# Hybrid DeltaNet/MLA/MoE block: one-pass products in the router's waits, rotary keys doubled by DMA, the decays' series with one instruction a term

## Chip, cores and metric

One Trainium2 chip, one core. The metric is the device time of one execution in microseconds, as the median of the runs. Engines are named as in the profile: PE is TensorE, PEld its weight loads, DVE is VectorE, ACT is ScalarE, POOL is GpSimd, SP is SyncE, which issues most DMAs.

## What is computed

A block of a bidirectional encoder over 512 tokens of 1024 features, in fp32: a gated DeltaNet (8 heads, both directions, chunks of 64) and a latent attention (MLA, 8 heads) side by side, merged by sigmoid gates, then a mixture of 16 experts in which each expert takes its 64 highest-scoring tokens. Cut to what the change touches:

```python
# MLA: one rotary key for all heads
q = rms_norm(c_q, q_gain) @ w_uq
k_rope = apply_rope(k_r, cos, sin)
# DeltaNet: decay per token and head
g = -exp(a_log) * softplus(a + dt_bias)          # cumulated within a chunk, then exp(differences)
# experts choose tokens
aff = softmax(h @ w_router)
gate, idx = top_k(aff.T, 64)                     # per expert
xe = h[idx]
hid = silu(xe @ w_gate) * (xe @ w_up)
ye = (hid @ w_down) * gate
out = zeros.at[idx].add(ye)
```

## The kernel before

Everything lies transposed, features on partitions and 512 tokens along the free axis, so that one product of 128 weights by 512 tokens fills a PSUM bank. A product at high accuracy is `mm3`: both factors are split into a high and a low part (ACT writes the high part, DVE or POOL the low one) and three one-pass products are accumulated. Where an operand is plain fp32, one product shows as two instructions in the trace.

The framework fixes the order of each engine's queue when the kernel is built: among what it thinks ready, the instruction that is earlier in the program goes first. Each engine works through its queue in that order. Tiles of one name take turns in a fixed number of buffers, in program order; the default PSUM bank `mm` has two. `tc.issue_after(ins)` puts what is traced under it behind `ins` on the same engine. Under `tc.manual_schedule` an engine keeps the order of the program.

The stages in order of time, with the lines that the prediction steps through:

- **Latents and rotary key (L283 to L412).** `lat_half` projects the latents; L321 and L322 take the square root on ACT and the reciprocal on DVE for the key-value norm, L324 applies it. L330 writes the low half of the query latent `cq`. `kr_ps` (L338) holds the projected key (64 rows) and the DeltaNet's a and b (32 rows); ACT copies all 96 rows to `kr1` (L340) and sends the last 32 to DRAM (L342). L348 sums the squares `sqs` over partitions, ACT copies the sums to `rs` (L350), four transposes (L353) turn them into a column per token. Then a product with `twice` (two identities side by side, L343 to L345 and L363) writes the 64 key rows twice into a second `kr_ps`, because the rotary helper `rope` (L397) works on 128 rows. `stage_a` (L432) projects the queries of two heads, the rotary part first (L452).
- **Attention (L519).** Heads go through `stage_a`, `stage_b` and `stage_c`, one step apart.
- **DeltaNet projections (L685).** For keys, then queries: projection, convolution on DVE (L667, L669), Silu on ACT (L670). After the sixth key tile comes `decays` (L590): softplus by a series in L612 to L620, then `gu` (L628), which eight small products (L632) read.
- **Decay blocks (L745).** For each of four token tiles `t` and both types `ty`: POOL multiplies (L749), PE applies `Lbd` (L751, bank `pjb`), ACT exponentiates; then the products `gkq` (L765). The framework merges them into the query projections.
- **Inverses, chunk steps, merge, output projection (L777 to L1300).**
- **Router (L1180 to L1377).** For each token tile `t`, while the next tile's output projection runs: transposes, logits with a fold product (`sum`, L1201), softmax, a transpose of the scores (L1227), then eight rounds of max and replace on DVE (`largest`). For the last tile PE has nothing else to do. `thr16` (L1324) is transposed (L1355), compared, and `counts` gives each token its place by bf16 products with `upto` and `ones_b`. `group` writes the one-hot tiles `OG` (L1393), `gather` multiplies them with the tokens (L1408).
- **Experts (L1543 on).** Weights come in quarters of 1 MB through a ring of 17 buffers (`ring`, L990); once the ring is full, the next load waits for the products that read the oldest quarter. The loops at L1543 and L1555 run gate, up and down products for the 16 experts.

Of the kernel before, what the change touches and what calls it, by code (L numbers as in the profile page):

```python
# [40 lines left out]
def block_kernel(ctx: ExitStack, tc: tile.TileContext, x, c, positions, w_mod, b_mod, g_mix, w_in, conv_w,  # L41
# [45 lines left out]
    def mm(o, lhsT, rhs, start=True, stop=True):  # L87
        return pe.matmul(o, lhsT, rhs, start=start, stop=stop)  # L88

    def mm3(o, lh, ll, rh, rl, start, stop):  # L90
# [251 lines left out]
    act.dma_start(ba_d, kr1[64:96])  # L342
    twice = mp("twice", 128)  # L343
    for i in range(2):
        dve.tensor_copy(twice[:64, 64 * i:64 * i + 64], ident[:64, :64])  # L345
    ss = lat[0]
    for i in range(4):
        mm(ss[32 * i:32 * i + 32], ones[:, 0:32], sqs[:, i])  # L348
    rs = tmp("rs", "t1")
    act.activation(rs, ss, AF.Copy)  # L350
    ss = lat[1]
    for t in range(4):
        turned_ = pe.transpose(ss[:, 128 * t:128 * t + 128], rs[:, 128 * t:128 * t + 128], ident)  # L353
    scq = mp("scq", 4)
# [5 lines left out]
    pm = Region("pmla", space=PSUM)  # L360
    kr_ps = bank("kr")
    with tc.issue_after(turned_.ins):
        mm(kr_ps, twice[:64], kr1[:64])  # L363

# [43 lines left out]

    kr = rope(kr_ps, True)
    tap("kr", kr)  # L410
# [179 lines left out]
    def decays():  # L590
# [24 lines left out]
        dve.tensor_tensor(t_[3], t_[2], t_[2], op=OP.mult)  # L615
        dve.tensor_scalar(t_[4], t_[3], 1.0 / 17, 1.0 / 15, op0=OP.mult, op1=OP.add)
        for n in (13, 11, 9, 7, 5, 3, 1):
            dve.tensor_tensor(t_[4], t_[4], t_[3], op=OP.mult)
            dve.tensor_scalar(t_[4], t_[4], 1.0 / n, None, op0=OP.add)
        dve.tensor_tensor(t_[4], t_[4], t_[2], op=OP.mult)  # L620
        dve.scalar_tensor_tensor(t_[4], t_[4], 2.0, t_[1], op0=OP.mult, op1=OP.add)
# [123 lines left out]
    for t in range(4):  # L745
        Dt = []
        for ty in range(2):
            gM = dp("gM", 512, bufs=2)
            pool.tensor_tensor(h8(gM), bh8(Mpk[ty]), b64(gu[:, ty, t]), op=OP.mult)  # L749
            psd = bank("pjb", 1, pp_)  # L750
            mm(psd, Lbd[ty], gM)  # L751
            Dx, Di = dp("Dx", 512, bufs=4), dp("Di", 512, bufs=4)
# [6 lines left out]
        for g in range(2):  # L759
            pv = bank("gkq", 2, pp_).rearrange("p (h e n) -> p h e n", h=4, e=2)  # L760
            hs = slice(4 * g, 4 * g + 4)
            for h in range(4):
                for cc in range(2):
                    q = slice(64 * cc, 64 * cc + 64)
                    mm(pv[q, h], kf[4 * g + h][:, t, cc], kq[4 * g + h][:, t, 2 * cc:2 * cc + 2][:, ::1 - 2 * cc])  # L765
            for e in range(2):
                for ty in range(2):
                    D_ = h8(Dt[ty][e])
                    dst = nAv(ty, t) if e == 0 else D_
                    dve.tensor_tensor(dst[:, hs], pv[:, :, e], D_[:, hs], op=OP.mult)  # L770
# [409 lines left out]
    class Logits:  # L1180
# [20 lines left out]
        def sum(self):  # L1201
            lT = dp("lT", 128)
            act.copy(lT, self.lg[:, :128])
            mm(self.lg[:, 128:144], lT, fold)
            return self.lg[:, 128:144]
# [5 lines left out]
    def scored(t):  # L1211

        a, m, s_, r_ = aff[:, t, :], stt[:, t, 0:1], stt[:, t, 1:2], stt[:, t, 2:3]
        lg = L[t].sum()
        act.activation(tbl[:, 1:2], rs[:, t:t + 1], AF.Exp, scale=0.0)
        dve.scalar_tensor_tensor(a, lg, rs[:, t:t + 1], c16, op0=OP.mult, op1=OP.add)
# [9 lines left out]
        pa = L[t].lg[:16, 256:384]  # L1226
        pe.transpose(pa, a, ident)  # L1227
        if t == 2:
# [131 lines left out]
    dve.tensor_tensor(eq, aff, b4(pth[:, :16]), op=OP.is_equal)  # L1360

    def counts(v, w=None):

# [6 lines left out]
        for i, (c, l, r) in enumerate(terms):  # L1370
            mm(ps[:, c], l, r, i == 0, i == len(terms) - 1)
        return ps[:, :64].rearrange("p (t e) -> p t e", t=4)
# [67 lines left out]
    for j in range(2):  # L1440
        ahead[j] = halves_of(j)
    group(0)
    gather(0, 0, 1)
    gather(0, 1, 1)
# [239 lines left out]
```

## Time and profile before

| | us |
|---|---|
| median of 3 runs | 1306.71 |
| lowest and highest run | 1306.16, 1306.81 |
| the profiled execution | 1305.51 |
| its span, first to last instruction | 1303.7 |
| PE busy in the span | 1225.3 (94%) |
| DVE, ACT, POOL busy | 668.7, 473.4, 314.5 |
| HBM read | 308.42 MB |

Times in the rows are microseconds from the start of the span unless marked ns. A timeline row gives start, duration, engine, line, operation, output and inputs, shape, and a count where neighbours of one kind are merged; in square brackets stands the idle time before it and what ended it. L88 is the line of the product helper `mm`, so that its rows are told apart by their tiles. PE's matmuls overlap, so the spacing of starts says more than durations. PEclk is the clock granted to PE: 1.00 is 2.4 GHz, 0.50 is 1.2 GHz.

### The profile page before, as it was taken

The numbers are of one execution on the slowest core, as the hardware profiler recorded it, in microseconds if no ns is written. First come the engines' busy times: TensorE is split into PE (matmuls) and PEld (weight loads), VectorE is DVE, ScalarE is ACT, GpSimd is POOL, SyncE is SP. The second block draws the span as 40 slices with busy tenths as digits, with TensorE's granted clock in tenths as the row PEclk, the third lists the DMA queues.
The fourth block names the chain that finished last, engine by engine and source line by source line (L and its number), as shares of the span: only waits on it lengthen the run. The fifth ranks groups of instructions, "written<-read, shape, count | busy, mean of one in ns | idle before, by whom it ended". The sixth has DMA issues, their size and how long they took to land.

```text
span 1303.7 us, 18255 instructions
## 1 busy us (share of the span) xinstructions
PE 1225.3 (94%) x6911; PEld 767.0 (59%) x6911; DVE 668.7 (51%) x1306; ACT 473.4 (36%) x986; POOL 314.5 (24%) x264
## 2 busy tenths in 40 slices
PE   5999999999999999999999999699999999999895
PEld 3767777667667777777877776333433443343233
DVE  4577776475669925945686766412222312223125
ACT  4455655556533346335631336410201110021003
POOL 2221210233544452434332242300300110020003
PEclk9989999999999999999999999799999999999998
DMA  9421222754363578585489773799999999999995
GB/s 353 121 63 41 71 88 70 232 178 138 121 186 97 180 195 230 168 235 170 161 295 316 249 257 140 285 379 421 421 420 420 421 421 420 421 420 421 420 414 185
DMA packets 153842, 333.82 MB, mean 256 GB/s; under 512 B 44864, under 2 KB 104462, under 8 KB 128794
## 3 DMA queue, kind: packets, MB, share of 16 engines
q1 hardware_dynamic: 130048, 308.75, 64.1%
q10 hardware_dynamic: 23370, 23.50, 5.7%
q8 instruction: 54, 0.88, 0.3%
q0 software_dynamic: 336, 0.41, 0.2%
q14 instruction: 34, 0.28, 0.1%
HBM read 308.42 MB, written 24.20 MB: 255 GB/s over the span
## 4 chain that ended last, share of the span: by engine, by line
PE 34%; DMA 22%; DVE 4%; ACT 2%; issue 1%; POOL 0%; SPq 0%; DVEq 0%; ACTq 0%; POOLq 0%
PE mm L88 11%; DMA exw<-in_w_down_dram 8%; DMA exw<-in_w_gate_dram 6%; PE wg L88 5%; DMA exw<-in_w_up_dram 4%; PE dnp L88 3%; PE wu L88 3%; PE po L88 2%; PE sc L88 2%; PE I L88 2%; PE Y L88 1%; DMA kq<-kq_d 1%; PE Q L88 1%; PE S L88 1%; DMA wraw<-in_w_o_dn_dram 1%
## 5 line engine op out<-in xcount | busy, mean ns | idle before, releaser
L88 PE MATMUL mm<-hT,wh 128*128 128x512 f32 (+1 forms) x656 | 218.5, 410 | 2.8 <-ACT wh L99 2.1
L96 POOL TENSOR_TENSOR wl<-wraw,wh 128x512 fp32r<-128x512 f32 (+1 forms) x88 | 126.8, 1457 | 254.8 <-ACT wh L99 236.9
L88 PEld LDWEIGHTS mm<-hT,wh 128*128 128x128 f32 (+1 forms) x656 | 122.4, 191 | 43.0 <-issue 9.5
L88 PE MATMUL mm<-hT,wl 128*128 128x512 f32 (+1 forms) x328 | 133.3, 406 | 3.8 <-POOL wl L96 3.7
L99 ACT ACTIVATE wh<-wraw 128x512 fp32r<-128x512 f32 (+1 forms) x138 | 86.5, 650 | 120.1 <-PE mm L88 58.0
L88 PE MATMUL wg<-exw,xe 128*64 128x512 f32 x512 | 121.8, 602 | 3.8 <-DMA exw<-in_w_gate_dram 2.5
L88 PE MATMUL wu<-exw,xe 128*64 128x512 f32 x512 | 117.8, 598 | 1.9 <-DMA exw<-in_w_up_dram 1.9
L96 POOL TENSOR_TENSOR xl<-xs,xh 128x512 fp32r<-128x512 f32 x32 | 40.2, 1273 | 307.3 <-ACT xh L1384 307.3
L1541 DVE TENSOR_TENSOR ye<-dnp,gt 64x512 f32<-64x512 f32 x30 | 20.7, 689 | 134.1 <-PE dnp L88 118.2
L1482 DVE TENSOR_TENSOR xa<-sc,xa 128x512 f32<-128x512 f32 x56 | 38.5, 691 | 88.4 <-PE sc L88 88.4
L88 PEld LDWEIGHTS mm<-hT,wl 128*128 128x128 f32 (+1 forms) x328 | 62.4, 190 | 22.4 <-POOL wl L96 6.0
L88 PEld LDWEIGHTS wu<-exw,xe 128*64 128x64 f32 x512 | 34.6, 137 | 65.6 <-issue 56.1
L88 PEld LDWEIGHTS wg<-exw,xe 128*64 128x64 f32 x512 | 33.6, 137 | 65.7 <-issue 55.0
L96 DVE TENSOR_TENSOR wl<-wraw,wh 128x512 fp32r<-128x512 f32 (+2 forms) x50 | 40.0, 811 | 39.5 <-ACT wh L99 28.9
L88 PE MATMUL po<-W,am 128*128 128x512 f32 x192 | 50.3, 406 | 0.8 <-DVE W L96 0.6
L793 DVE TENSOR_TENSOR pr<-lanT,nl 128x1 f32<-128x1 f32 (+30 forms) x62 | 43.7, 704 | 1.6
L667 DVE SCALAR_TENSOR_TENSOR cv<-mm,vecT,cv 128x510 f32<-128x510 f32 (+1 forms) x32 | 23.8, 743 | 35.7 <-ACT cv L663 35.4
L88 PE MATMUL mm<-am,wh 128*128 128x512 f32 x128 | 41.2, 399 | 0.0
L1607 POOL TENSOR_TENSOR xa<-xa,late 128x256 f32<-128x256 f32 (+1 forms) x16 | 10.7, 706 | 125.6 <-DMA late<-in_g_final_dram 125.6
L88 PEld LDWEIGHTS po<-W,am 128*128 128x128 f32 x192 | 34.4, 188 | 11.1 <-issue 1.6
L88 PE MATMUL mm<-oz,wh 128*128 128x512 f32 x128 | 40.6, 398 | 0.0
L88 PE MATMUL mm<-OG,xh 128*128 128x256 f32 x128 | 34.2, 304 | 2.8 <-DVE OG L1393 2.8
(597 smaller groups left out, 2399.7 us busy)
## 6 DMA issues: line engine op xcount, KB each, us to landing
exw<-in_w_gate_dram SPq DMA_DIRECT2D x64, 1024.0 KB
exw<-in_w_up_dram SPq DMA_DIRECT2D x64, 1024.0 KB
exw<-in_w_down_dram SPq DMA_DIRECT2D x63, 1024.0 KB
wraw<-in_w_in_dram SPq DMA_DIRECT2D x38, 512.0 KB
wm<-in_w_mod_dram SPq DMA_DIRECT2D x32, 512.0 KB
wraw<-in_w_in_dram ACTq DMA_DIRECT2D x16, 512.0 KB
xa<-in_w_mod_dram SPq DMA_DIRECT2D x16, 512.0 KB
kq<-kq_d SPq DMA_DIRECT2D x7, 1024.0 KB
```

The source lines that it names most:

```text
L88: return pe.matmul(o, lhsT, rhs, start=start, stop=stop)
L96: eng.tensor_tensor(o, a, b, op=OP.subtract)
L99: act.activation(hi, src, AF.Copy)
L667: dve.scalar_tensor_tensor(cv[:, -s:], ps[:, :512 + s], w(d), cv[:, -s:], op0=OP.mult, op1=OP.add)
L793: dve.tensor_tensor(pv, T3[:, 0:i, 0:i], nb, op=OP.mult)
L1482: dve.tensor_tensor(y[t][:, c:c + 512], ps, y[t][:, c:c + 512], op=OP.add)
L1541: dve.tensor_tensor(ye[o_, c], ps[64 * q:64 * q + 64, :], gt2[64 * q:64 * q + 64, c], op=OP.mult)
L1607: pool.tensor_tensor(y[t][:, cs], y[t][:, cs], gfin[:, cs], op=OP.mult)
```

## The change

Five edits.

1. A helper `awake` issues `n` products of `upto` (bf16, 128x128) with `ones_b` broadcast to 512 columns into a PSUM tile that nobody reads, behind a given PE instruction. It is used four times: 4 behind `decayed` (the second `Lbd` product of token tile 0), 6 behind the last tile's fold product, 24 behind the transpose of its scores, 6 behind the last product of `counts`.
2. `twice` and its product go. ACT copies the 64 key rows to a new tile `kr2` and a DMA from ACT's queue copies the same rows of `kr1` to its upper half; `rope` reads `kr2` from SBUF, no longer a PSUM bank.
3. The copy of the sums to `rs` is DVE's, no longer ACT's.
4. The series in `decays` takes one fused instruction a term: add the constant, multiply.
5. `Logits.sum` and `counts` keep their last product, so that `awake` can be put behind it.

```diff
+    def awake(o, n, behind=None):
+
+        with tc.issue_after(behind.ins) if behind is not None else nullcontext():
+            for _ in range(n):
+                mm(o[:, :512], upto, ones_b[:, None, :].to_broadcast([128, 4, 128]))
...
     act.dma_start(ba_d, kr1[64:96])
-    twice = mp("twice", 128)
-    for i in range(2):
-        dve.tensor_copy(twice[:64, 64 * i:64 * i + 64], ident[:64, :64])
+    kr2 = mp("kr2", 512)
+    act.activation(kr2[:64], kr_ps[:64], AF.Copy)
+    act.dma_start(kr2[64:128], kr1[0:64])
...
-    act.activation(rs, ss, AF.Copy)
+    dve.tensor_copy(rs, ss)
     ss = lat[1]
     for t in range(4):
-        turned_ = pe.transpose(ss[:, 128 * t:128 * t + 128], rs[:, 128 * t:128 * t + 128], ident)
+        pe.transpose(ss[:, 128 * t:128 * t + 128], rs[:, 128 * t:128 * t + 128], ident)
...
-    kr_ps = bank("kr")
-    with tc.issue_after(turned_.ins):
-        mm(kr_ps, twice[:64], kr1[:64])
...
-    kr = rope(kr_ps, True)
+    kr = rope(kr2, True)
...
         dve.tensor_scalar(t_[4], t_[3], 1.0 / 17, 1.0 / 15, op0=OP.mult, op1=OP.add)
+        dve.tensor_tensor(t_[4], t_[4], t_[3], op=OP.mult)
         for n in (13, 11, 9, 7, 5, 3, 1):
-            dve.tensor_tensor(t_[4], t_[4], t_[3], op=OP.mult)
-            dve.tensor_scalar(t_[4], t_[4], 1.0 / n, None, op0=OP.add)
-        dve.tensor_tensor(t_[4], t_[4], t_[2], op=OP.mult)
+            dve.scalar_tensor_tensor(t_[4], t_[4], 1.0 / n, t_[3 if n > 1 else 2], op0=OP.add, op1=OP.mult)
...
-            mm(psd, Lbd[ty], gM)
+            decayed = mm(psd, Lbd[ty], gM)
...
             hs = slice(4 * g, 4 * g + 4)
+            if t == 0 and g == 0:
+                awake(pv.rearrange("p h e n -> p (h e n)"), 4, decayed)
...
-            mm(self.lg[:, 128:144], lT, fold)
+            self.last = mm(self.lg[:, 128:144], lT, fold)
...
         lg = L[t].sum()
+        if t == 3:
+            rest = bank("po", 2, px)
+            awake(rest, 6, L[t].last)
...
-        pe.transpose(pa, a, ident)
+        done = pe.transpose(pa, a, ident)
+        if t == 3:
+            awake(rest, 24, done)
...
-            mm(ps[:, c], l, r, i == 0, i == len(terms) - 1)
+            counted.append(mm(ps[:, c], l, r, i == 0, i == len(terms) - 1))
...
     group(0)
+    awake(bank("wg", 1, pe_), 6, counted[-1])
     gather(0, 0, 1)
```

## Rows read from the trace of the kernel before

**Rows 1.** The page: its span, and PE's granted clock in 40 slices (tenths).
```profile
span 1303.7 us, 18255 instructions
PEclk9989999999999999999999999799999999999998
```
**Rows 2.** Busy time by stretch; the columns are named in the first line.
```profile
core 0: us, PE busy (x) PEld busy (x) DVE busy (x) ACT busy (x) POOL busy (x), PEclk, DMA share, GB/s
79.20:85.90 6.70, 6.70 (x14) 3.85 (x14) 5.02 (x10) 1.90 (x4) 2.52 (x2) 0.50 0.22 59
294.00:297.50 3.50, 3.50 (x12) 2.92 (x12) 2.39 (x5) 0.38 (x1) 1.52 (x2) 0.52 0.00 0
297.50:309.00 11.50, 11.50 (x58) 8.13 (x57) 3.05 (x11) 9.12 (x16) 0.61 (x1) 1.00 0.31 93
334.00:348.50 14.50, 14.50 (x74) 10.01 (x72) 8.55 (x12) 9.02 (x16) 9.14 (x8) 1.00 0.39 131
828.00:837.00 9.00, 8.30 (x36) 5.45 (x37) 1.70 (x3) 1.72 (x3) 2.54 (x2) 0.70 0.08 15
828.70:832.40 3.70, 3.70 (x18) 3.48 (x18) 1.00 (x2) 0.69 (x2) 0.84 (x1) 0.50 0.00 0
832.40:836.50 4.10, 4.10 (x17) 1.45 (x16) 0.00 (x0) 1.02 (x2) 1.70 (x2) 0.88 0.00 0
860.00:1275.00 415.00, 404.94 (x1882) 154.93 (x1878) 94.60 (x161) 56.18 (x93) 30.16 (x24) 1.00 1.01 419
```
**Rows 3.** Timeline of PE from 76 to 83.5 us.
```profile
78.60 0.71 PE L353 MATMUL lat<-ident,rs 128*128 128x128 f32 x4 [3.09 <-ACT rs L350]
79.24 2.07 PE L88 MATMUL mm<-kr,twice 64*128 64x512 f32 x2
81.24 1.22 PE L88 MATMUL mm<-cq,uqh 128*128 128x512 f32 x2
```
**Rows 4.** Timelines of DVE and ACT from 72 to 83 us.
```profile
73.35 0.74 DVE L330 SCALAR_TENSOR_TENSOR cq<-lat,vecT,cq 128x512 fp32r<-128x512 f32 x1
76.14 3.35 DVE L322 RECIPROCAL rs<-rs 128x512 f32<-128x512 f32 x1 [2.04 <-ACT rs L321]
79.41 1.16 DVE L96 TENSOR_TENSOR wl<-wraw,wh 128x1024 fp32r<-128x1024 f32 x1
80.49 1.28 DVE L324 TENSOR_TENSOR ckvf<-ckvf,rs 128x512 f32<-128x512 f32 x2
...
75.42 0.69 ACT L321 ACTIVATE rs<-mm,eps 128x512 f32<-128x512 f32 x1
```
**Rows 5.** Groups of DVE's instructions from 281.7 to 291.9 us: the series.
```profile
L619 DVE TENSOR_SCALAR sp<-sp 128x64 f32<-128x64 f32 x7 | 3.3, 472 | 0.2
L618 DVE TENSOR_TENSOR sp<-sp,sp 128x64 f32<-128x64 f32 x7 | 2.3, 331 | 0.1
```
**Rows 6.** Timeline of PE from 288 to 298 us.
```profile
289.21 0.63 PE L88 MATMUL mm<-hT,wh 128*128 128x512 f32 x2
289.67 0.40 PE L88 MATMUL mm<-hT,wl 128*128 128x512 f32 x1
292.32 0.38 PE L88 MATMUL tok<-gu,Mbd 128*128 128x32 f32 x2 [2.25 <-DVE gu L628]
```
**Rows 7.** Timeline of PE from 816 to 838 us.
```profile
816.98 0.39 PE L88 MATMUL lg<-fold,lT 128*128 128x16 f32 x2 [0.39 <-ACT lT L1203]
819.25 0.28 PE L1227 MATMUL lg<-ident,aff 128*16 128x128 f32 x1 [1.88 <-DVE aff L1223]
825.60 0.28 PE L1355 MATMUL mm<-ident,thr 16*128 16x16 f32 x1 [6.07 <-DVE thr L1324]
828.70 0.77 PE L88 MATMUL mm<-OG,xh 128*128 128x256 f32 x2 [1.76 <-DVE OG L1393]
...
836.86 0.28 PE L88 MATMUL mm<-OG,xh 128*128 128x256 f32 x1
836.97 0.28 PE L88 MATMUL mm<-OG,xl 128*128 128x256 f32 x1
```
**Rows 8.** Groups of ACT's instructions from 300 to 366 us: table loads for Exp.
```profile
L753 ACT ACT_TABLE_LOAD x3 | 3.8, 1283 | 0.1
```

More of the change, by code (lines that the diff above doesn't have):

```diff
@@ L1 @@
-from contextlib import ExitStack
+from contextlib import ExitStack, nullcontext
 import numpy as np
@@ L1360, in block_kernel @@
     dve.tensor_tensor(eq, aff, b4(pth[:, :16]), op=OP.is_equal)
+    counted = []
     def counts(v, w=None):
```

## The prediction, made before the changed kernel was run

> **What bounds the kernel now.** I read the page first: the span and the granted clock of TensorE in 40 slices [rows 1]. The span is 1303.7 us, and the profiled execution took 1305.51 us, so 1.8 us lie around the span; the median of the runs shown, 1306.71 us, is 1.2 us above that execution. All sums below are made against 1305.51 and moved up by 1.2 at the end. The slices say that the clock is full nearly everywhere (2.4 GHz); the places where it sinks to half (1.2 GHz) are few, so the next view is busy time by stretch. From 860 to 1275 us the DMA engines are full (share 1.01, 419 GB/s) and TensorE is busy 405 of 415 us [rows 2]: the experts are a stream of weights. Between 828 and 837 that stream stands still (share 0.08): the 17 quarters that fit are loaded, and the next load needs the first quarter to be used up. So whatever brings the first expert products forward restarts the stream as much earlier, and the end of the kernel with it. Before the experts TensorE is the engine that is nearly always busy, and what it loses at one place it hardly gets back. Hence the reading order from here: where TensorE waits, and how long the half clock lasts behind each wait. Three such places lie beside the change: 75.5 to 85.9 us (latents and rotary key), 290 to 297.5 (decays), and 817 to 836 (router).
>
> **Rotary key.** TensorE ends the sums over sqs at 75.51 and waits 3.09 us for ACT's copy of them [rows 3]. ACT was late: its square root of L321 began at 75.42 [rows 4], and a weight split and the copy of kr stood between that and the copy of the sums. Behind the wait the clock is at half from 79.2 to 85.9 [rows 2]. In that stretch stands the product with `twice`, from 79.24 to 81.24, that is 2.0 us, and the query's rotary product cannot start before 81.24 [rows 3].
> The change takes the `twice` product off TensorE, adds on ACT one copy of 64 rows and one DMA issue, and moves the copy of the sums from ACT to DVE. The ceiling of the gain: the copy runs on DVE at once when the sums are there. DVE is idle from 74.1 to 76.14 [rows 4], and a pass of 512 columns takes it 0.64 (half of L324's 1.28), so the transposes come at 76.2 instead of 78.60: 2.4; the `twice` product: 2.0; and the 4.66 us from 81.24 to 85.9 at full clock: 2.3. Together 6.7 us. The floor: DVE takes L322's reciprocal first (it is earlier in the program), which holds DVE from 76.14 to 79.49; then the weight split and L324, which end at 81.77 [rows 4], and only then the copy. The transposes would start at 82.5, the query's products at 83.2 instead of 81.24, and the half clock would last some 2 us longer: 3.0 us lost.
> I expect the copy behind the reciprocal, since both wait for work that ends within 0.7 us and the reciprocal is earlier in the program; but I don't expect TensorE to stand for all of it. The query's 12 products have their inputs (the last cq is done at 74.09 [rows 4]), and they are no longer queued behind the `twice` product. Of the two banks that take turns in the program, they now get the one that the square root frees at 76.11, no longer the one that kr's copy frees. At 0.23 us each [rows 6] they fill 76.15 to 78.9 if all stand ahead of the transposes (then some 5 us are gained), and 76.15 to 76.85 if only three do (then TensorE waits for 80.2 all the same, and 1.3 us are gained). I take 3.0 us gained, between the two; bounds 6.7 gained and 3.0 lost.
> The upper half of kr2 comes by DMA, in the place of 2.0 us of TensorE. ACT issues it behind kr's copy, where the copy of the sums stood that let the transposes go at 78.60 [rows 3], and its reader on ACT has splits ahead of it that wait for L324's end at 81.77 [rows 4]. So some 3 us hide it at no cost; a landing later than that would hold up the key's chain one for one, and how long ACT's queue takes to land is not in the trace. I take nothing, within the bounds above. The Trainium skill gives about 2.0 us as the fixed cost of one transfer on GpSimd's path (DMA: Bandwidth & Descriptors, Anatomy of one DMA — SWDGE (gpsimd) path); if ACT's takes no longer, it lands by an estimate near 80.6, before its reader, and the sum is the same.
>
> **Decays.** The series on DVE is 15 instructions: 7 multiplies of 2.3 us in total, 7 additions of 3.3, one last multiply of about 0.2 [rows 5], together 5.8. They lead to gu, and TensorE, whose last product starts at 289.67, waits 2.25 us for it [rows 6]. Then it runs at half clock from 294 to 297.5 (0.52) [rows 2]: 3.5 us of work that takes 1.75 at the full clock. The change makes it one multiply and seven fused instructions, 8 in all. At the multiplies' mean of 0.33 that is 2.6, so gu comes 3.2 us earlier; bounds from seven instructions of 0.2 (1.4) to eight at 0.225 (4.0). Above 2.25 the wait is gone and the clock has no reason to fall: 2.25 + 1.65 = 3.9 us gained. At 1.4 the wait is cut by 1.4 and the fall may stay, so the bounds are 1.4 and 4.0. What is late next: for 11.5 us behind it TensorE is busy all the time with DVE at 3.05 of 11.5 [rows 2], so nothing near takes the gain back.
>
> **Four products behind `decayed`.** Between 334 and 348.5 TensorE is busy all 14.5 us [rows 2], and the second decay product lies in there, so the four find no gap: 4 x 0.23 = 0.9 us. Part of it is hidden, since TensorE next waits for an ACT chain that began before them. I take 0.5 lost. If they came to lie in a wait and kept the clock up they could save up to 1.6 (half of some 3 us); at the half clock they would cost 1.7. They also tie the first gkq products behind them.
>
> **Router.** The fold product of the last quarter ends at 817.37, the transposed scores at 819.53, and then TensorE stands 6.07 us until the threshold is there at 825.60, and 1.76 us until OG at 828.70 [rows 7]. It comes back at half clock: the two gathers run from 828.70 to 832.40 at 0.50, 0.21 us a product [rows 2], where later ones take 0.12 (836.86 to 836.97) [rows 7]. No one-pass bf16 product of 512 columns is in the trace. The nearest row is a 512-column product at full clock, 0.23 us from start to start [rows 6]; the other end is twice that, 0.46, at the half clock. At 0.23 the six take 1.4 us and end at 818.8, ahead of the scores at 819.25; the 24 take 5.5 and end at 825.05, ahead of the threshold at 825.60; the last six end at 828.35, ahead of OG. So all of it lies in waits, and what stands behind each (the threshold's transpose, the gather) isn't delayed.
> With the clock held: the 16 gather products save 16 x 0.09 = 1.45, the first two quarters' products 0.5 (0.12 of 4.1 us, at a clock of 0.88) [rows 2], the counts 0.1. So the first quarter is free 2.1 us earlier, the stream restarts 2.1 us earlier, and the end follows. Bounds: 0 to 2.3 gained, unless the 24 run over (rival B).
>
> **Sum.** 3.0 + 3.9 - 0.5 + 2.1 = 8.5 us gained: 1305.5 - 8.5 = 1297.0, and with the 1.2 us to the median **1298.2 us**.
>
> **Rivals.**
> A. TensorE stands before the transposes behind DVE's reciprocal. For it: the order of a queue is fixed when the kernel is built, and a 3.35 us reciprocal now stands in the way where there was none. Rotary gain 0 instead of 3.0: 1301.2; with the floor, 1304.2.
> B. The 24 products don't hold the clock. They then take 24 x 0.46 = 11.0 us, to 830.6; the threshold's transpose queues 5.0 us behind them, the last six run 1.0 over, and gather and products run at half as now. 6.0 lost instead of 2.1 gained: 1306.3, which is no change. Against it: with them TensorE is busy from 817.4 to 825.05 but for half a us, where without them it stood. The Trainium skill says that matmuls stay in program order and only weight loads are pulled ahead (TensorE: Matmul & The Clock Gate, Step-by-step: what each phase is for): a product nobody reads is an obstacle, and any overrun beyond 825.60 counts in full.
> C. Slower: the decay products spread among the last projections. ACT switches tables between Exp and Silu, 1.28 us a load; between 300 and 366 it did so for Exp three times [rows 8]. The edge behind `decayed` and the shorter series put these products at other points of the queue. Each added pair of loads is 2.57 us on ACT, with TensorE waiting for the Silu that follows. From four added pairs (10.3) on the whole gain is gone; five make 1298.2 + 12.8 = 1311. Against it: only eight such blocks exist, and the trace packs them together.
> D. DVE copies at once and the whole rotary gain comes: 3.7 us more, 1294.5.
>
> **How the numbers follow.** Forecast (gain of 5.5 to 11) 0.55; A 0.20; B 0.10; C 0.07; D 0.08. About 0.2% (2.6 us) is what a measurement of this kernel can tell from no change. Faster: the forecast, A but for its floor, and D: 0.81. Within 0.2%: most of B and A's floor: 0.11. Slower: C and the worst of B: 0.08. The range reaches from just under D's time, with the decays at their best, to near B's: 1293.5 to 1306.
>
> **What would show it.** Rotary: no `twice` product; TensorE's wait before the transposes under 1.5 us and no half clock near 80 to 86; wrong if it stands until DVE's reciprocal is done. Decays: the wait for gu gone, clock full at 290 to 300. Router: clock full from 817 to 836, the gather at 0.12 us a product, the threshold's transpose waiting for DVE and not for the products ahead of it, the DMA gap shorter by some 2 us on its late side. The prediction is wrong if the gains show in these places and the end doesn't follow, or if the stretch from 300 to 366 has more table loads.

## The result, and the profile after

The changed kernel takes 1298.98 us in the median of its runs (1297.92 to 1300.29), beside 1306.56 us for the kernel before (1306.16 to 1306.81): a ratio of 0.9935, 95% interval 0.9914 to 0.9956, or 7.6 us gained. The prediction was 1298.2 us with a range of 1293.5 to 1306. So the time came out as forecast. Of the four terms of the sum only the decays came out in size and in the main for the reason given; two were too large, and one came by accident. Most of what follows is about that.

The profiled execution of the changed kernel is the slowest of its runs, 1300.29 us. Its page, the span and the granted clock in 40 slices, beside [rows 1]:

```profile
span 1298.5 us, 18322 instructions
PEclk9999999999999999999999999999999999999997
```

The two slices that had sunk in [rows 1], an 8 at 65 to 98 us and a 7 at 815 to 847, are back at 9; half clock is still there, in shorter stretches. By stretch (the columns as in [rows 2]):

```profile
82.00:87.00 5.00, 2.91 (x9) 2.52 (x10) 3.79 (x8) 2.53 (x5) 2.51 (x2) 0.67 0.31 79
280.00:300.00 20.00, 19.11 (x91) 14.44 (x89) 14.16 (x30) 10.88 (x18) 8.29 (x8) 0.91 0.25 74
812.00:813.50 1.50, 0.44 (x9) 0.17 (x9) 1.45 (x8) 1.14 (x5) 0.00 (x0) 1.00 0.78 300
813.50:816.00 2.50, 2.50 (x9) 1.10 (x10) 2.17 (x11) 2.47 (x5) 0.00 (x0) 0.63 1.01 426
814.00:817.00 3.00, 3.00 (x10) 1.11 (x9) 2.38 (x14) 2.96 (x7) 0.00 (x0) 0.52 1.04 431
825.00:831.50 6.50, 6.33 (x36) 3.75 (x34) 1.86 (x4) 1.72 (x3) 2.50 (x2) 1.00 0.02 5
860.00:1270.00 410.00, 401.33 (x1860) 153.78 (x1856) 94.78 (x161) 55.59 (x92) 30.16 (x24) 1.00 1.01 419
```

The stream of weights still fills the DMA engines from 860 us on (1.01, 419 GB/s), and the gap ahead of it still is there (0.02 from 825 to 831.5), but it ends sooner. The three places that the prediction spoke of, on TensorE in order of time (start, duration, what it is, in brackets the idle time before it and what ended it):

```profile
77.83 0.73 PE L88 MATMUL mm<-cq,uqh 128*128 128x512 f32 x2 [0.70 <-ACT rs L327]
...
80.03 0.63 PE L88 MATMUL mm<-cq,uqh 128*128 128x512 f32 x2
84.09 1.11 PE L359 MATMUL lat<-ident,rs 128*128 128x128 f32 x4 [3.43 <-DVE rs L356]
...
288.21 0.39 PE L88 MATMUL mm<-hT,wl 128*128 128x512 f32 x1
289.48 0.38 PE L88 MATMUL tok<-gu,Mbd 128*128 128x32 f32 x2 [0.88 <-DVE gu L630]
...
813.49 0.39 PE L88 MATMUL lg<-fold,lT 128*128 128x16 f32 x2 [0.39 <-ACT lT L1207]
813.73 2.35 PE L88 MATMUL po<-ones_b,upto 128*128 128x512 bf16 x6
815.87 0.42 PE L1234 MATMUL lg<-ident,aff 128*16 128x128 f32 x1
816.08 6.08 PE L88 MATMUL po<-ones_b,upto 128*128 128x512 bf16 x24
823.37 0.22 PE L1364 MATMUL mm<-ident,thr 16*128 16x16 f32 x1 [1.21 <-DVE thr L1333]
...
825.96 0.48 PE L88 MATMUL mm<-OG,xh 128*128 128x256 f32 x2 [0.17 <-DVE OG L1404]
...
831.96 0.39 PE L88 MATMUL mm<-OG,xh 128*128 128x256 f32 x1
```

Beside [rows 3, 6, 7]: the wait ahead of the four transposes is 3.43 us instead of 3.09, though eleven of the query's products now stand in front of it; the wait for gu is 0.88 instead of 2.25; the wait for the threshold is 1.21 instead of 6.07. The third gather starts at 831.96 (the last row above); in the kernel before it was this row:

```profile
836.51 0.39 PE L88 MATMUL mm<-OG,xh 128*128 128x256 f32 x1
```

### The profile page after: what moved, and what is told of

It reads as the page before. It is cut to its first block, busy times and chain, and to the rows that moved or that the text cites. A ratio compares the mean times of both kernels' runs of the same rounds, so it can differ in the third digit from the quotient of the medians.

```text
span 1298.5 us, 18322 instructions
## 1 busy us (share of the span) xinstructions
PE 1232.3 (95%) x6949; PEld 770.7 (59%) x6949; DVE 665.8 (51%) x1298; ACT 474.8 (37%) x987; POOL 313.2 (24%) x264
## 4 chain that ended last, share of the span: by engine, by line
PE 40%; DMA 16%; DVE 4%; ACT 1%; issue 1%; POOL 0%; DVEq 0%; ACTq 0%; SPq 0%; POOLq 0%
PE mm L88 14%; DMA exw<-in_w_down_dram 6%; PE wg L88 6%; DMA exw<-in_w_gate_dram 5%; DMA exw<-in_w_up_dram 5%; PE wu L88 4%; PE dnp L88 4%; PE po L88 3%; PE sc L88 2%; PE I L88 2%; PE Y L88 1%; PE Q L88 1%; PE S L88 1%; PE V L88 1%; DMA kq<-kq_d 1%
## 5 line engine op out<-in xcount | busy, mean ns | idle before, releaser
L88 PEld LDWEIGHTS mm<-hT,wh 128*128 128x128 f32 (+1 forms) x656 | 122.5, 190 | 40.6 <-issue 8.5
L88 PEld LDWEIGHTS sc<-yh,OHT 128*128 128x128 f32 x56 | 10.4, 186 | 43.9 <-issue 42.2
```

## Stages, in all the profiles of this study

One pair of profiles tells little of terms of 1 to 4 us. The experiments left twelve more, and in most of them a given stage is unchanged, either as before or as after. So here is each profile cut at the same seven instructions. The columns are worked out from the starts of these instructions: A from the first product over sqs to the sums over the squares of L697 (pja<-sq, near 258 us); B from there to the second of the two groups tok<-ident,kc near 300; C to the last block of gkq products (near 365); D to the last tile's fold product; E to the third gather; F to the first down product of the last expert but one (dnp<-exw,late), which stands for the end: some 38 us follow it in every profile.

| kernel | A | B | C | D | E | F |
|---|---|---|---|---|---|---|
| before | 183.6 | 44.2 | 65.5 | 449.3 | 19.5 | 429.2 |
| e1_router | 184.1 | 45.4 | 65.7 | 449.2 | **18.5** | 428.3 |
| e2_series | 184.2 | **39.9** | **69.9** | 453.2 | 19.3 | 428.2 |
| e3_rotary | **183.5** | 45.5 | 64.1 | 449.5 | 19.3 | 428.4 |
| e4_decayed | 184.4 | 44.0 | **67.3** | 448.4 | 19.6 | 428.3 |
| after, first profile | **182.0** | **41.5** | **64.3** | 449.6 | **18.5** | 428.6 |
| f1_after | **182.0** | **39.9** | **64.3** | 450.3 | **18.5** | 428.4 |
| f2_series_decayed | 184.2 | **41.5** | **67.0** | 447.5 | 19.7 | 428.5 |
| f3_no_decayed | **181.3** | **41.5** | **70.0** | 449.2 | **17.8** | 428.7 |
| h1_order_only | **183.8** | **39.9** | **66.0** | 450.3 | **18.5** | 428.2 |
| e5_copy_first | **182.3** | **39.9** | **64.3** | 448.5 | **17.8** | 428.6 |
| g1_copy_first_xs_pool | **182.4** | **39.9** | **67.2** | 448.6 | **17.7** | 428.2 |
| e9_48 | **183.3** | **39.9** | **67.0** | 449.0 | **21.4** | 428.9 |
| e7_no_first6 | **183.8** | **41.8** | **65.4** | 449.1 | **18.7** | 428.6 |

Bold is a stage that the kernel in that row changes. Three things can be read from it at once. F is nearly the same for all (428.2 to 429.2): what is won before the third gather arrives whole at the end. B has two levels with the short series, 39.9 and 41.5: at 39.9 the clock between 280 and 300 us is full, at 41.5 it is 0.91. And C is worst where the series is there without the four products (69.9, 70.0); with both it is 64.3 to 67.2, with neither 64.1 to 65.7. A good part of these differences goes with the clock. In C it falls to half not at all, once or twice: not at all in e3_rotary, after, f1_after, e5_copy_first and e7_no_first6 (C 64.1 to 65.4), once in before, e1_router, e4_decayed, f2_series_decayed, h1_order_only and e9_48 (65.5 to 67.3), twice in e2_series, f3_no_decayed and g1_copy_first_xs_pool (67.2 to 70.0).

## The experiments

### The four parts alone

Does the gain consist of the parts? Each of these four is the kernel before with one part of the change.

e1_router, the 6, 24 and 6 products alone:

```diff
+            rest = bank("po", 2, px)
+            awake(rest, 6, L[t].last)
...
+            awake(rest, 24, done)
...
+    awake(bank("wg", 1, pe_), 6, counted[-1])
```

> The kernel before with the 6, 24 and 6 products in the router's waits alone. Theory from the two traces: the clock comes back while the products run and the gathers run at 0.12 us a product (2.3 us gained from the threshold to the third gather), but the threshold itself comes 1.2 us later, because the products delay the scores' transpose by some 0.1 us and DVE's last step of two SBUF operands then starts just after POOL's split and takes 1.2 instead of 0.2 us. Net 1.1 us gained: 1305.5. Rival 1, the prediction's term: 2.1 gained, 1304.5, fold product to threshold no longer than 8.7 us. Rival 2: the clock in this place decides nothing and the end stays at 1306.6.

Measured: 1305.62 us beside 1306.97, ratio 0.9992 (0.9982 to 1.0002). The profile has the theory's numbers: E is 18.5 instead of 19.5, the threshold's transpose comes 9.89 us behind the fold product (8.62 before), the gather product takes 0.12 us. The time is where the theory put it, but the interval takes in no change and the prediction's 2.1 as well; what speaks for the theory is E, 1.0 shorter.

e2_series, the fused series alone:

```diff
-            dve.tensor_tensor(t_[4], t_[4], t_[3], op=OP.mult)
-            dve.tensor_scalar(t_[4], t_[4], 1.0 / n, None, op0=OP.add)
+            dve.scalar_tensor_tensor(t_[4], t_[4], 1.0 / n, t_[3 if n > 1 else 2], op0=OP.add, op1=OP.mult)
```

> The kernel before with the fused series alone. Theory from the two traces: gu comes some 2.8 us earlier, TensorE still waits 0.9 us for it and the clock still falls behind that wait; 2.6 us gained: 1304.0. Rival, the prediction's term: wait and half clock both gone, 3.9 gained, 1302.7.

Measured: 1307.05 us, ratio 1.0009 (0.9992 to 1.0026). Both theories fail. B is 39.9 instead of 44.2, so the gain is there, and more of it than the theory said; C then takes 69.9 instead of 65.5 and gives it back. (D is some 4 us longer than in the other profiles; this execution, at 1310.04, is 3 us above the median, and why is open.) TensorE stands at 366.12 for DVE's Di (two fences, TensorE and DVE of this kernel):

```profile
366.12 1.62 PE L88 MATMUL gkq<-kq 128*64 128x128 f32 x16 [2.80 <-DVE Di L769]
```
```profile
361.20 3.45 DVE L755 TENSOR_TENSOR Dx<-Dx,nbeta 128x512 f32<-128x512 f32 x2
```

e3_rotary, the key by DMA and the copy on DVE alone:

```diff
+    act.dma_start(kr2[64:128], kr1[0:64])
...
-    act.activation(rs, ss, AF.Copy)
+    dve.tensor_copy(rs, ss)
```

> The kernel before with the rotary key doubled by DMA and the copy of the sums on DVE alone. Theory from the two traces: TensorE works through the query's products and then stands some 3 us before the four transposes, since DVE takes the reciprocal, a weight split and a key-value scaling ahead of the copy; 1.7 us gained: 1304.9. Rival 1, the prediction's term: 3.0 gained, 1303.6. Rival 2, the prediction's case A: nothing gained, 1306.6.

Measured: 1306.52 us, ratio 1.0005 (0.9987 to 1.0023); TensorE stands 3.44 us ahead of the transposes, as in the changed kernel. A is 183.5; the five profiles with the old code have 183.6 to 184.4. The run can't tell 1.7 gained from nothing; the prediction's 3.0 lies outside its interval.

e4_decayed, the four products alone:

```diff
+            if t == 0 and g == 0:
+                awake(pv.rearrange("p h e n -> p (h e n)"), 4, decayed)
```

> The kernel before with the four products behind the second decay product alone. Between 300 and 813 us the changed kernel gained 0.9 us that no term of the prediction stands for. Theory: the four products hold the clock between 340 and 360 us (0.91 before, 1.00 after) and gain about 0.9: 1305.7. Rival 1, the prediction's term: 0.5 lost, 1307.1. Rival 2: the 0.9 came from the earlier decays, or from chance, and the products change nothing: 1306.6, clock between 340 and 360 still near 0.91.

Measured: 1309.29 us, ratio 1.0013 (1.0000 to 1.0025), with C at 67.3 instead of 65.5. The theory of a gain of 0.9 is wrong; the prediction's 0.5 lost lies within the interval. Multiplied, the four ratios make 1.0019: measured alone, the parts add up to no gain, where all of them together gave 0.9935.

### Which two act on each other

f1_after is the changed kernel once more, beside the next three.

> The changed kernel itself, so that the next three and the four parts have it beside them on one chip. The parts alone gave 1.4 us gained (router), 0.1 lost (series), 0.4 gained (rotary), 2.3 lost (four products): together nothing. If the parts add up, the changed kernel takes some 1306 us here; if they act on each other, it takes 7 to 8 us less than the kernel before, about 1299, as in its first runs.

Measured: 1300.29 us beside 1308.06, ratio 0.9940 (0.9923 to 0.9957). The parts act on each other.

f2_series_decayed is the kernel before with the diffs of e2_series and e4_decayed together.

> The kernel before with the fused series and the four products, without router and rotary. Theory: the shorter series alone gains its 3.9 us before 302 us and loses 4.4 again between 302 and 368, where the decay blocks stand at other points of the queues: TensorE waits 2.8 us before a block of products for DVE's Di, and the clock sinks to 0.84 between 350 and 370. The four products move the first block of gkq products behind the second decay product (from 309 to 339 us) and with that the later blocks; that wait is 0.6 us in the changed kernel and the clock full. So both together gain 5 to 6 us: 1301 to 1302. Rival 1: the parts add up: 0.1 and 2.3 lost, 1309. Rival 2: the products act by holding the clock, not by the order of the queues: then the wait for Di stays over 2 us and the clock is full all the same.

Measured: 1303.31 us, ratio 0.9965 (0.9950 to 0.9980), 4.7 us gained, where the two alone gained nothing and lost 1.7. So the parts don't add up (rival 1). For rival 2 the clock would have to be full; it is 0.91 from 350 to 370, and the wait for Di is 1.72, between the two theories. One correction to the text above: what moves from 309 to 340 us is the first four gkq products, not the whole block.

f3_no_decayed takes the four products out of the changed kernel:

```diff
-            if t == 0 and g == 0:
-                awake(pv.rearrange("p h e n -> p (h e n)"), 4, decayed)
```

> The changed kernel without the four products behind the second decay product. Theory as for the run above: 4 to 6 us slower than the changed kernel, about 1304, the loss between 302 and 368 us with a wait of over 2 us for Di. Rival, the prediction's term: 0.5 us faster than the changed kernel, about 1298.5.

Measured: 1305.27 us, ratio 0.9981 (0.9965 to 0.9996), 5.0 us slower than f1_after on the same chip, intervals apart. C is 70.0 beside 64.3. With the series shortened, the four products are worth 5 us. How, is to be seen by laying the two side by side where they part. Without the products, TensorE, DVE and POOL:

```profile
364.17 1.25 PE L88 MATMUL gkq<-kq 128*64 128x128 f32 x9 [2.81 <-DVE Di L772]
```
```profile
359.24 3.45 DVE L758 TENSOR_TENSOR Dx<-Dx,nbeta 128x512 f32<-128x512 f32 x2
362.62 0.74 DVE L772 TENSOR_TENSOR nA<-gkq,Dx 128x256 f32<-128x256 f32 x2
```
```profile
359.15 1.31 POOL L756 TENSOR_TENSOR Di<-Dx,Mpk 128x512 f32<-128x512 f32 x1 [0.56 <-DMA int_d<-Di]
360.72 1.42 POOL L756 TENSOR_TENSOR Di<-Dx,Mpk 128x512 f32<-128x512 f32 x1 [0.26 <-ACT Dx L755]
```

With them (f1_after):

```profile
359.63 1.09 PE L88 MATMUL gkq<-kq 128*64 128x128 f32 x16 [0.64 <-DVE Di L774]
```
```profile
356.87 1.29 DVE L758 TENSOR_TENSOR Dx<-Dx,nbeta 128x512 f32<-128x512 f32 x2
```
```profile
358.71 2.51 POOL L756 TENSOR_TENSOR Di<-Dx,Mpk 128x512 f32<-128x512 f32 x2 [2.49 <-DMA int_d<-Di]
```

The same two DVE multiplies take 1.29 us when POOL is idle and 3.45 when POOL's multiply began 0.09 us ahead of them (359.15 and 359.24): 2.2 us, and the wait for Di behind them is longer by as much (2.81 and 0.64). With the products, POOL's next multiply starts at 358.71, 0.55 us after DVE's two are done; here it waits for a buffer of Di to be written out. These 2.2 us are not the whole 5.7 by which the two differ in C. The other large part is the granted clock (f3_no_decayed twice, then f1_after):

```profile
347.50:351.00 3.50, 3.45 (x20) 2.86 (x21) 3.50 (x7) 0.00 (x0) 0.79 (x1) 0.56 0.09 31
363.50:368.50 5.00, 4.33 (x35) 3.28 (x35) 5.00 (x13) 0.00 (x0) 0.00 (x0) 0.66 0.28 105
```
```profile
346.80:364.00 17.20, 16.56 (x133) 10.28 (x134) 15.97 (x34) 2.89 (x5) 8.29 (x7) 1.00 0.45 119
```

Without the products TensorE runs at half clock behind a wait of 1.60 us for Di that ends at 347.55 (1.12 with them), and again behind the 2.81. Step by step the 5.7 are: 0.4 up to the end of that first wait, 1.6 at half clock behind it, 2.2 in the wait above, 1.6 at half clock behind that. So without the products two waits are longer, one of them by POOL beside DVE, and the half clock follows both. Whether the products' own work helps to keep the clock, this pair can't tell.

h1_order_only puts an edge in the place of the products:

```diff
-                awake(pv.rearrange("p h e n -> p (h e n)"), 4, decayed)
...
+                    with tc.issue_after(decayed.ins) if t == 0 and g == 0 else nullcontext():
                         mm(pv[q, h], kf[4 * g + h][:, t, cc], kq[4 * g + h][:, t, 2 * cc:2 * cc + 2][:, ::1 - 2 * cc])
```

> The changed kernel with the first block of 16 gkq products put behind the second decay product, but without the four products nobody reads. Theory: what counts is that this block no longer stands among the first items of the stage, so that the later decay blocks stand closer together; then the wait for Di is under 1.2 us and the time is that of the changed kernel, 1300. Rival 1: the work of the four products counts, by keeping the clock: then without them the clock sinks between 330 and 370 and the time is about 1305, as without the edge. Rival 2: it is the exact order that came out with the four products: then it may end anywhere between, with the wait for Di showing it.

Measured: 1301.75 us beside 1307.54, ratio 0.9953 (0.9941 to 0.9964). That is most of the way from f3_no_decayed (0.9981) to f1_after (0.9940), without a single product that nobody reads. Rival 2 describes it best: the wait for Di is 1.27, the two multiplies take 2.36, C is 66.0. The order counts. It doesn't give everything: rival 1 has a point too, since the clock does fall once without the products (0.54 from 348.5 to 352, behind a wait of 1.59 for Di, as in f3_no_decayed), and that is the larger part of the 1.7 us by which C is above 64.3. But the clock falls there in f2_series_decayed, g1_copy_first_xs_pool and e9_48 too, which have the products and a wait of 1.1. So what the products' own work adds, if anything, stays open. The two multiplies also differ among kernels of one kind: with both parts in, they take 1.28 to 1.29 us in three profiles (C 64.3) and 2.36 to 2.39 in three (f2_series_decayed, g1_copy_first_xs_pool, e7_no_first6; C 65.4 to 67.2); in the seventh, e9_48, a multiply just ahead of them is late instead. What sets this, and the clock, from one execution to the next stays open.

### The rotary key

e5_copy_first, the changed kernel with the copy ahead of the reciprocal:

```diff
-            dve.reciprocal(rs, rs)
...
+    copied = dve.tensor_copy(rs, ss)
+    with tc.issue_after(copied.ins):
+        dve.reciprocal(rk, rk)
```

(with the two multiplies by it and the split of the key-value latents moved behind it)

> The changed kernel with DVE's reciprocal for the key-value norm and what follows from it put behind the copy of the sums. Theory: TensorE's 3.4 us before the four transposes go, and the half clock behind them; DVE's copy comes at about 77.5 us of that run, and the query's products follow without a gap: 2 to 3 us faster than the changed kernel, 1296 to 1297. Rival 1: the key-value latents come 1 to 2 us later, TensorE waits for them before 95 us instead, and nothing is gained: 1299. Rival 2: the other order of the queues in the attention costs more than that: over 1300.

Measured: 1297.52 us beside 1308.06, ratio 0.9924 (0.9904 to 0.9943). DVE's queue now stands as wanted, but for one weight split that is still ahead of the copy, and TensorE's wait is 1.61 instead of 3.43:

```profile
79.00 0.65 PE L361 MATMUL lat<-ident,rs 128*128 128x128 f32 x4 [1.61 <-DVE rs L353]
```
```profile
77.12 1.23 DVE L102 TENSOR_TENSOR wl<-wraw,wh 128x1024 fp32r<-128x1024 f32 x1 [2.99 <-ACT wh L105]
78.26 0.68 DVE L353 COPY rs<-lat 128x512 f32<-128x512 f32 x1
78.86 3.34 DVE L355 RECIPROCAL rs<-rs 128x512 f32<-128x512 f32 x1
```

The clock from 80 to 100 us is full. But A is 182.3, where the changed kernel has 182.0 in both its profiles: of 1.8 us less waiting and a full clock nothing can be seen at 258 us. Rival 1 fits (TensorE waits 0.80 for the key-value latents and 0.45 for kn before 95 us). But the seven profiles with the change's order have 181.3 to 183.8 there, so a gain of a part of it is not excluded. In the two profiled executions, 2.7 us apart, the difference lies in other stages (E 17.8, D 448.5), and the two intervals overlap: a gain is not shown.

### The router

e9_48, the changed kernel with twice as many products ahead of the threshold:

```diff
-            awake(rest, 24, done)
+            awake(rest, 48, done)
```

> The changed kernel with 48 instead of 24 products behind the transpose of the scores. Theory: TensorE takes its products in program order, so the 24 more (24 x 0.24 = 5.7 us) run past the threshold, which TensorE waits 0.9 to 1.4 us for in the changed kernel: the threshold's transpose and the end come 4.3 to 4.8 us later, 1304.5 to 1305. Rival: what is ready goes ahead of products that nobody reads, or the experts' stream takes the loss up: 1300 to 1301.

Measured: 1303.25 us beside 1307.54, ratio 0.9968 (0.9953 to 0.9982), against 0.9940 for the changed kernel: some 3.7 us lost by the medians' ratios, though the two intervals just touch. E is 21.4, where it is 17.7 or 17.8 in the kernels with the clock full at the fold product as here. TensorE:

```profile
817.27 10.52 PE L88 MATMUL po<-ones_b,upto 128*128 128x512 bf16 x48
827.73 0.23 PE L1364 MATMUL mm<-ident,thr 16*128 16x16 f32 x1
```

The transpose has no wait left ahead of it; it starts when the 48th product is done, 12.85 us behind the fold product, where e5_copy_first, with the clock full at the fold product as here, has 8.62. So it comes in order, and 4.2 us late. Of these 0.55 come back, since DVE's sum of places (slt) behind a later threshold no longer meets POOL (2.60 us from the transpose to the first gather, where f3_no_decayed has 3.15).

e7_no_first6, without the six behind the fold product:

```diff
-            awake(rest, 6, L[t].last)
```

> The changed kernel without the six products behind the fold product. Theory: at half clock (0.39 us each) the six end behind the scores and delay their transpose by 0.1 to 0.3 us, which puts DVE's last step behind POOL's start; without them the threshold comes 8.6 us behind the fold product instead of 9.9, and the third gather 17.8 instead of 18.5: 0.7 us faster, 1299.6. Rival: without them the clock is still at half when the 24 begin and comes back only late in them; then they run over, 24 x 0.43 = 10.3 us, the threshold's transpose comes over 11 us behind the fold product, and it is 1302 or more.

Measured: 1302.21 us, ratio 0.9949 (0.9933 to 0.9965), the same as the changed kernel within the intervals. The theory is wrong in the profile:

```profile
817.87 0.38 PE L1233 MATMUL lg<-ident,aff 128*16 128x128 f32 x1 [1.88 <-DVE aff L1229]
818.04 7.75 PE L88 MATMUL po<-ones_b,upto 128*128 128x512 bf16 x24
825.73 0.22 PE L1363 MATMUL mm<-ident,thr 16*128 16x16 f32 x1
```

Behind 1.88 us of standing the 24 start at the half clock (0.59 from 815 to 821) and take 7.75 us instead of 5.34 (e5_copy_first); the threshold is ready at 824.26 and its transpose waits for the products, to 10.14 us behind the fold product. So the six spare the 24 some 2.4 us where the clock is full, but in time that is not shown to pay: E is 18.7 here and 18.5 in the changed kernel, where the six are late themselves.

g1_copy_first_xs_pool, e5_copy_first with one of ACT's two xs tiles given to POOL:

```diff
-        if t % 2:
+        if t == 1:
             act.activation(xs[:, :, t], v, AF.Copy, scale=rs[:, t:t + 1])
```

> The changed kernel with the reciprocal behind the copy of the sums (as in the run before last of this study, 2.8 us faster than the changed kernel) and with one more of the four router inputs xs written by POOL, one fewer by ACT. Theory: ACT and POOL then finish xs, xh and xl some 2 us earlier, POOL's split no longer runs beside DVE's last small steps, and from the fold product of the last tile to the third gather it takes 17.2 us or less, where it took 18.5 in the changed kernel and 17.8 where the clock was full: 0.5 us faster than without this edit, 1297.0. Rival: POOL's extra 3.9 us beside DVE's residual sums between 800 and 815 us slow those by as much: 1297.5 or more, with the stretch from the third to the fourth fold product longer than 7.9 us.

Measured: 1300.17 us beside 1307.54, ratio 0.9931 (0.9912 to 0.9950): no gain over e5_copy_first. E is 17.7 instead of the 17.2 hoped for. POOL's split does start earlier against the fold product (6.2 us behind it, 8.3 in e5_copy_first), and now meets another of DVE's steps (POOL, then DVE):

```profile
819.58 2.49 POOL L102 TENSOR_TENSOR xl<-xs,xh 128x512 fp32r<-128x512 f32 x2 [2.47 <-ACT xh L1397]
```
```profile
821.45 0.69 DVE L1256 TENSOR_TENSOR top<-top,top 16x64 f32<-16x64 f32 x1
```

The rival is wrong too: from the third to the fourth fold product it takes 7.94 us, as in the kernel before.

## Why the prediction was right, step by step

**The end follows TensorE.** Right. F is 428.2 to 429.2 in all fourteen profiles, while the third gather starts anywhere from 827 to 842.

**Rotary key: 3.0 predicted.** A is 183.6 to 184.4 in the five profiles with the old code (mean 184.1) and 181.3 to 183.8 in the seven with the change's (mean 182.8): 1.3 gained. That DVE takes the reciprocal first was called rightly:

```profile
77.81 3.35 DVE L328 RECIPROCAL rs<-rs 128x512 f32<-128x512 f32 x1 [2.04 <-ACT rs L327]
81.08 1.16 DVE L102 TENSOR_TENSOR wl<-wraw,wh 128x1024 fp32r<-128x1024 f32 x1
82.16 1.28 DVE L330 TENSOR_TENSOR ckvf<-ckvf,rs 128x512 f32<-128x512 f32 x2
83.35 0.68 DVE L356 COPY rs<-lat 128x512 f32<-128x512 f32 x1
```

So was the filling: eleven of the query's products go ahead of the transposes. But the sum took the copy to come right behind the reciprocal (79.49 and one pass, 80.2), and gave no reason why the weight split and L324 of its floor should not stand between. They do: the transposes come 8.0 us behind the start of the sums over sqs, as the floor had it (82.5, where the sums start at 74.45). What failed beside that is the step from the filling to the gain. Eleven products of 0.23 us fill 2.5 us of a stand of some 7, TensorE still stands 3.43 in one piece, and the clock falls behind it as it did before (0.67 from 82 to 87). "Under 1.5 us and no half clock near 80 to 86" is wrong in the changed kernel, and by the prediction's own sign (TensorE stands until the reciprocal is done) the step is wrong. The low figure of that step, 1.3, which it gave for a case with fewer products, is what came, by luck. In e5_copy_first the stage is not seen to be shorter even without the long stand: the key-value latents are late next. Rival A was half right: TensorE does stand behind the reciprocal, but that costs the gain only in part. The DMA for the key's upper half cost nothing, as the sum had it: its first reader in the changed kernel (DVE at 85.33, issue at 79.92) does not wait for it. In e5_copy_first, where ACT reads early, ACT stands until 80.37, 2.4 us from the start of the issue at 77.97:

```profile
80.37 0.63 ACT L105 ACTIVATE rx<-kr 128x512 fp32r<-128x512 f32 x1 [2.33 <-DMA kr<-kr]
```

**Decays: 3.9 predicted.** B is 44.0 to 45.5 with the long series (mean 44.8) and 39.9 to 41.8 with the short one (ten profiles, mean 40.6): 4.2 gained. The size is right, one reason isn't: the wait for gu did not go, it is 0.86 to 0.95 in all ten. The order of the queue is fixed when the kernel is built, and with a shorter series the eight small products were given a place further ahead: the last product in front of them starts at 288.21 instead of 289.67 [rows 6]. What was counted as a wait saved came as work moved behind. The clock falls behind the short wait in four of the ten profiles (B 41.5 to 41.8) and not in the other six (39.9), so the 4.2 is a mean of two levels.

**Four products behind `decayed`: 0.5 lost predicted.** This step failed, though its number came. Alone they lose 1.7 (e4_decayed, interval 0 to 3.3); with the series they gain 5.0 (f1_after and f3_no_decayed). The prediction took the series' 3.9 as safe because DVE had room just behind it, and priced the products by their own 0.9 us. Rival C did say that both put the decay products at other points of the queue, but priced that by table loads alone; what the order does to DVE, POOL and the clock 50 us later had no term. By the table, series and products together leave C at 65.6 (mean of seven), and the kernels with neither have 65.1 (mean of three): 0.5 lost for the pair. The number is the one predicted for the products, by an accident of two errors: the series alone would have given back 4.8 of its gain.

**Router: 2.1 predicted.** E is 19.5 without the products (mean of five) and 18.5 in the changed kernel, 17.7 to 17.8 in three others: 1.0 and 1.7 gained. The gathers were sized well: first to third gather takes 6.00 us instead of 7.81 [rows 7], 1.8 gained where the sum had 1.95. What was missed lies ahead of them. The prediction took the clock as full while the six run. In the first profile of the changed kernel it is full up to the fold product (1.00 from 812 to 813.5) and falls while the six run (0.63 from 813.5 to 816); in f1_after it falls just ahead of the fold product. So the six took 2.35 and 2.72 us instead of 1.4 and ended behind the scores, not ahead of them. That delays the transpose of the scores by 0.1 us here and 0.7 in f1_after, and this small delay has a price of its own (DVE, then POOL, of the changed kernel):

```profile
821.84 1.23 DVE L1254 TENSOR_TENSOR top<-top,top 16x64 f32<-16x64 f32 x1
```
```profile
821.73 2.48 POOL L102 TENSOR_TENSOR xl<-xs,xh 128x512 fp32r<-128x512 f32 x2 [12.89 <-ACT xh L1395]
```

In the kernel before the same two were:

```profile
825.09 0.21 DVE L1245 TENSOR_TENSOR top<-top,top 16x64 f32<-16x64 f32 x1
```
```profile
825.19 2.49 POOL L96 TENSOR_TENSOR xl<-xs,xh 128x512 fp32r<-128x512 f32 x2 [12.86 <-ACT xh L1384]
```

There DVE's step began 0.10 us ahead of POOL's split. Now it begins 0.11 behind the split and takes 1.23. With the clock full (e5_copy_first) it is ahead again, 0.21, and E is 17.8. Rival B did not come in the changed kernel; e7_no_first6 shows a piece of it.

**Rivals C and D.** Between 300 and 366 us the Exp table is loaded three times, as before [rows 8], and in the whole kernel one load more stands ahead of a Silu (6 instead of 5): no mishap of that size. D did not come; DVE does not copy at once.

**The sum.** By the means of the table the changed kernel gains 1.3 + 4.2 - 0.5 + 1.0, that is 6.0; 7.6 to 7.8 were measured. The rest isn't settled. F is 0.6 to 0.8 shorter than in the kernel before, but it is as short in e2_series, e3_rotary, e4_decayed and f2_series_decayed, so that is no gain of the change. The changed kernel's own two profiles, against the same means of the others, give 2.1 + 4.1 + 0.8 + 1.0, that is 8.0: there C is 64.3, shorter than with neither part, where by the seven it is longer. Two profiles can't tell which is nearer its median. 8.5 was predicted, and the single terms are off by -1.7, +0.3, 0 and -1.1. So the time was hit with terms that err by up to 1.7 us and mostly one way, and with one interaction of some 6.5 us in C (series alone 4.8 lost, products alone 2.2 lost, both 0.5 lost) that no term names and that falls out well for the change. That the sum is as near as 0.8 us is luck; that the end follows TensorE, and the size of the decays, are not.

## What to carry to other kernels

Where a program's queues are laid out by a scheduler, an edit that is worth 4 us where it is made can move the order of work 50 us later and lose them there, in longer waits and in the half clock behind them: compare the built order of all engines, not only the edited lines, and measure parts together as well as alone. Products nobody reads pay only in a wait that is as long as they are, at the clock that they will start with; count them at the half clock too, and look for what a small delay of the chain beside them runs into. When a wait has been filled, ask what stands behind the filling before a gain is booked: here other late inputs came next, and of 1.8 us nothing could be seen at the end of the stage.

## What the runs showed of the hardware

**DVE and POOL exclude each other for whole instructions.** A DVE instruction with two operands in SBUF that starts while POOL works on SBUF does its work behind the end of POOL's instruction, as the runs show for two sizes. With 64 columns it ends 0.07 to 0.10 us behind that end; with 512 columns (0.69 alone) 0.55 us behind it, as the second of f3_no_decayed's two multiplies (362.69) behind POOL's second (362.14). `top<-top,top` of 16x64 elements takes 0.21 us alone, and 1.23, 0.72 and 0.69 where POOL's split had 1.13, 0.62 and 0.62 left to run (the changed kernel, f1_after, g1_copy_first_xs_pool; each of the two splits in a row taken as half of 2.48 or 2.49). The sum of places (slt) in e5_copy_first is the same case (POOL, then DVE):

```profile
817.72 2.49 POOL L102 TENSOR_TENSOR xl<-xs,xh 128x512 fp32r<-128x512 f32 x2 [12.91 <-ACT xh L1397]
```
```profile
818.97 0.22 DVE L1387 TENSOR_TENSOR slt<-mm,sel 128x64 f32<-128x64 f32 x1 [0.21 <-PE mm L88]
819.51 0.78 DVE L1390 TENSOR_TENSOR slt<-slt,tie 128x64 f32<-128x64 f32 x1
```

The first of these two has one operand in PSUM and keeps its 0.22 us beside the running POOL. The Trainium skill (SBUF — State Buffer, SBUF: two separate sides) states it so: the port pair that the two engines share is an exclusive lock, and whichever of them starts first has it for its whole instruction. The runs agree, and they show the consequence that I had not weighed: a shift of 0.2 us decides between 0.2 and 1.2.

**TensorE keeps to the order of its queue** also for products that nobody reads: with 48 of them the threshold's transpose waited 4.3 us past the threshold (ready at 823.45, taken at 827.73). The Trainium skill (TensorE: Matmul & The Clock Gate, Step-by-step: what each phase is for) says that matmuls stay in program order; the trace agrees.

**One-pass products bring the clock back and hold it.** Six of 512 columns take 1.46 us at full clock and 2.35 to 2.72 where it falls before or among them; after the 24 the gathers run at 0.12 us a product in every profile that has them. Whether the clock falls near the fold product, after waits of 0.4 to 0.8 us, differs from one execution to the next: just ahead of it in f1_after, among the six in the changed kernel's first profile, not at all in e5_copy_first. Why is open.
